# Moving the value products in the attention rounds, and turning two head outputs at a time in the scans

## The chip, the cores and the metric

The kernel runs on one core of one Trainium2 chip. The metric is the device time of one execution in microseconds. Before the change the median of three runs is 2172.1 us (2171.45 to 2173.77). The engines of a core work side by side and wait for each other through semaphores: TensorE (matrix products; PE in the profile, its weight loads PEld), VectorE (DVE), ScalarE (ACT), GpSimd (POOL), and SyncE (SP), whose queue here issues transfers.

## The reference

One encoder layer with two gated branches is applied to a batch of 1024 tokens (called A here) and one of 512 (B), with shared weights and width 1024, all in float32:

```python
h = rms_norm(x, pre_w);  cols = h @ w_in
# branch A: mLSTM with 4 heads of 256, forward and backward, in chunks of 128
num = (sc @ v) + wa * (q @ C);  h_t = num / max(|den|, exp(-m));  C = decay * C + kw.T @ v
y_m = headnorm(h_fwd + h_bwd) * sigmoid(o) * silu(z)
# branch B: 3 dilation groups (1, 4, 16) x 8 heads of 64, window +-64 steps of the dilation
p = exp(q @ k.T + bias - max);  o = p @ v;  y_a = (mix of the groups by their denominators) * silu(z_a)
merged = sig(g0) * (y_m @ w_pm) + sig(g1) * (y_a @ w_pa)
x + rms_norm(merged @ w_out, post_w)
```

## The kernel before

Products in full precision are made of three TensorE products of a high and a low part of each operand (`mm3`, lines 232 to 237). The first 960 us are the input projections of A. After them three kinds of work share TensorE: what A's and B's scans and attention need, step by step, and between these steps *projections* (tile `dense`: B's input projections, then the output projections). The projections come from a generator, `Fill`: `fill(x)` issues a share x of the steps that the stage is to take.

TensorE's and SP's instructions keep the order in which the code writes them (`manual_schedule`). The instructions of ScalarE, VectorE and GpSimd are put in order by a planner that simulates a timeline; `issue_after` ties single instructions behind others, and `self.held` is a list of the last four attention evictions and exponentials, behind which a weight split goes.

The four stages behind the input projections, in time: the scan of A (`mlstm`), the attention of A (`attend`), the scan of B (`quad`, beside which A's attention groups are combined), the attention of B. Then B's groups are combined and the output projections end the kernel.

**Scan rounds.** A round is a head, a chunk and a direction: 4 x 8 x 2 rounds for A, 4 x 4 x 2 for B. In A's round k, TensorE gets in order: a step of `prepare` for the next head, if one is due (six steps, in rounds 8 to 13 of the first three heads: scores `st`, line 1248, or four transpositions of keys, line 1257, each into a PSUM tile `a` that ScalarE empties, lines 1250 and 1258); a `turn`; a third of a share of projections; then `core(k)` with products `num` and `kv` and further projections. From the second half of the chunks on, `core` leaves a normalized head output `hn` (a ring of `late + 1` tiles) and a function `turn` for it: two transpositions into an `a` tile (line 1370), a product with G on VectorE (line 1372) into one of two `ym` tiles, and a write of it that the SP queue issues at the next round's `tick`. `late` is 4 for A and 3 for B: in round k the turn of round k - late runs. Tiles `a` have two PSUM banks, `num` two, `kv` one of two banks; two more are for projections. In B's scan the preparing steps go to another tile (`sc`), and `a` is shared with the combination's transpositions (line 2111). Turns left at the end run one by one with a share of projections each.

**Attention rounds.** `att_round` runs once for each tile of 128 queries and goes through a list of (age, stage): a stage of the tile that came so many rounds ago. Stages of a usual tile: 0 logits `lg` on TensorE (line 1848, or through `mm3`); 1 softmax (VectorE adds the bias and finds the maximum, ScalarE takes exponentials); 2 `turn`, transpositions into `pt` (line 1878) and their copy to `pts` by VectorE or ScalarE in turns; 3 the products with the values, `o`; 4, for A only, transposing back. The list has the place `(None, None)` for a share of projections.

For A, stage 3 is `columns`: only every fourth tile does it, for four tiles at once, with 32 products of 64 output rows (lines 1919 and 1921) and a copy `oT` by ScalarE; stage 4, `back`, turns `oT` (line 1931) and queues the writes. For B, stage 3 is `output`: four to eight products with 64 columns (line 1900; line 1893 for tiles that wrap around), a copy by ScalarE and a queued write for each tile. Tiles of the last dilation group, in both batches, are *compact*: their stages are attached to tiles under other numbers (line 1790), logits (line 1747) as stage 5 of age 0, transpositions (line 1770) as stage 6 of age 4, and their output (line 1779) as stage 3 of age 3. Tiles `lg`, `pt` and `o` have two PSUM banks each.

Of the kernel before, what the change touches and what calls it, by code (L numbers as in the profile page):

```python
# [206 lines left out]
class Net:  # L207
# [1006 lines left out]
    def mlstm(self, T, fill, steps, first, banks, lead, after, beside=()):  # L1214
# [7 lines left out]
        head, made, turns, rws = {0: first}, {}, {}, {}  # L1222
        beside, late = iter(beside), 4 if n > 4 else 3
        self.lag = 2 if n > 4 else 3
        with ExitStack() as stack:
# [150 lines left out]
            def load_G(h):  # L1376
                for c in range(2):
                    self.queue(("G", h), ("G", S, 2 * h + c), G[:, c], T.G[2 * h + c])
# [11 lines left out]
            for k, (h, i, d) in enumerate(rounds):  # L1390
                self.tick()
                if i == (n > 4) and d == (n <= 4):
                    if h < 3:
                        head[h + 1] = self.ml_load(T, h + 1)
                        self.spread(n - 2 if n > 4 else 1)
                    else:
                        after()
                        self.spread(2 * n - 4)
                if d == 0 and i == n // 2 and h < 3:
                    coming = prepare(h + 1)  # L1400
                if coming is not None and next(coming, coming) is coming:
                    coming = None
                if k % 4 < 2:
                    rows(k // 4 + 1, k % 4)
                if k + 1 < len(rounds):
                    with self.tc.issue_after(hold.ins) if k < 3 else ExitStack():
                        front(k + 1)
                self.sum = self.acc[1]
                turns.pop(k - late, lambda: None)()
                if h > 0 and i == 2 and d == 0:  # L1410
                    load_G(h)
                fill(1 / 3)
                core(k)
                self.sum = self.acc[1]
                for _ in range(1 if i < n - 1 else 2):
                    next(beside, None)
# [11 lines left out]
    def quad(self, T, fill, steps, first, after, beside):  # L1428
# [7 lines left out]
        head, made, turns, rws, col = {0: first}, {}, {}, {}, {}  # L1436
        beside, late, lead = iter(beside), 3, 2
        self.lag = 3
        with ExitStack() as stack:
# [157 lines left out]
            for k, (h, i, d) in enumerate(rounds):  # L1597
                self.tick()
                if i == d == 0 and h < 3:
                    qk = self.qk_load(T, h + 1)  # L1600
                    self.spread(1)
                if i == 0 and d == 1:
                    if h < 3:
                        head[h + 1] = self.ml_load(T, h + 1, qk)
                        self.spread(1)
                    else:
                        after()
                        self.spread(2 * n - 4)
                if i == d == 1 and h < 3:
                    coming = prepare(h + 1)  # L1610
                if coming is not None and next(coming, coming) is coming:
                    coming = None
                if k % 4 < 2:
                    rows(k // 4 + 1, k % 4)
                if k + 1 < len(rounds):
                    with self.tc.issue_after(hold.ins) if k < 3 else ExitStack():
                        front(k + 1)
                self.sum = self.acc[1]
                turns.pop(k - late, lambda: None)()
                if h > 0 and i == 2 and d == 0:  # L1620
                    load_G(h)
                fill(1 / 3)
                core(k)
                self.held = []
                self.sum = self.acc[1]
                next(beside, None)
# [98 lines left out]
    def compact(self, T, u, qkv, bias, sb):  # L1725

        nc, n = self.nc, T.n
        q, k, v = qkv
        og = T.og[:, 2, u % 4].rearrange("(i t b) w -> b i t w", t=n, b=2)
        bt = bias()[:, :P].rearrange("p (h w) -> p h w", h=2)  # L1730
        halves = [slice(64 * b, 64 * b + 64) for b in range(2)]
        for hh in range(2):
            e = self.erow[8 * (2 if n > 4 else 3) + 2 * (u % 4) + hh]
            for x in halves:
                self.queue(("table", u), None, bt[x, hh], bass.AP(tensor=e.tensor, offset=e.offset + 193, ap=[[1, 64], [1, 64]]))
        bt = bt[:, :, ::-1]

        def batch(b0):
            ts = {}
            of = lambda t, b: 64 * (2 * (b0 + t) + b)  # L1740

            def products():
                lg = ts["lg"] = self.bank("lg").rearrange("p a b -> p (a b)")
                for t in range(4):
                    for b, x in enumerate(halves):
                        c = slice(of(t, b), of(t, b) + 64)
                        nc.tensor.matmul(lg[x, t * P:(t + 1) * P], q[:, c], k[:, :, c], start=True, stop=True)

            def softmax(i):
                if i == 0:  # L1750
                    ts["st"] = sb.tile([P, 4, 4], F32, name="st", bufs=2)
                    ts["ls"] = sb.tile([P, 2, 256], F32, name="ls", bufs=3).rearrange("p a b -> p (a b)").rearrange(
                        "p (t h w) -> p t h w", t=4, h=2)
                lg = ts["lg"].rearrange("p (t h w) -> p t h w", t=4, h=2)[:, i]
                ls, st = ts["ls"][:, i], ts["st"][:, i]
                nm = sb.tile([P, 2], F32, name="nm", bufs=3)
                for hh in range(2):
                    nc.vector.tensor_tensor_reduce(out=ls[:, hh], in0=lg[:, hh], in1=bt[:, hh], scale=1.0, scalar=NEG, op0=OP.add,
                                                   op1=OP.max, accum_out=st[:, 2 + hh:3 + hh])
                nc.vector.tensor_scalar(nm, st[:, 2:4], -1.0, None, op0=OP.mult)  # L1760
                for hh in range(2):
                    self.held = self.held[-3:] + [nc.scalar.activation(ls[:, hh], ls[:, hh], AF.Exp, bias=nm[:, hh:hh + 1],
                                                                      accum_out=st[:, hh:hh + 1])]

            def turn(i):
                pp = self.bank("pt")
                if i == 0:
                    ts["pt"] = sb.tile([P, 4, P], F32, name="pts", bufs=5 if n > 4 else 2)
                for j in range(2):
                    nc.tensor.transpose(pp[:, j], ts["ls"][:, 2 * i + j].rearrange("p h w -> p (h w)"), self.ident)  # L1770
                pt = ts["pt"][:, 2 * i:2 * i + 2]
                self.held = self.held[-3:] + [nc.scalar.activation(pt, pp[:, :2], AF.Copy) if i else nc.vector.tensor_copy(pt, pp[:, :2])]

            def output():
                po = self.bank("o")
                for t in range(4):
                    for b, x in enumerate(halves):
                        c = of(t, b)
                        nc.tensor.matmul(po[x, t], ts["pt"][:, t, x], v[:, :, c:c + 64], start=True, stop=True)
                if b0 == n - 4 and u < 10:  # L1780
                    self.queued[:0] = self.values_of(T, u + 2, v)
                put = self.ot_batch()
                ot = put.rearrange("p (t w) -> p t w", w=OW)
                nc.vector.tensor_copy(ot[:, :, P:], ts["st"])
                self.held = self.held[-3:] + [nc.scalar.activation(ot[:, :, :P], po, AF.Copy)]
                for b, x in enumerate(halves):
                    self.put(("og", T.S), og[b, :, b0:b0 + 4], ot[x], put, lag=1)

            on = lambda f, *x: (lambda: f(*x))
            return [{6: on(turn, 0)}, {6: on(turn, 1)}, {5: products, 1: on(softmax, 1), 2: on(softmax, 3)},  # L1790
                    {0: on(softmax, 0), 1: on(softmax, 2), 3: output}]

        return [x for b0 in range(0, n, 4) for x in batch(b0)]

    def attention(self, T, u, qkv, bias, sb, ps):
# [257 lines left out]

    def att_round(self, tiles, fill):

        for age, stage in ((0, 0), (1, 1), (2, 2), (4, 4), (None, None), (3, 3), (0, 5), (4, 6)):
            if age is None:
                fill(1)
            elif age < len(tiles) and tiles[-1 - age] is not None and stage in tiles[-1 - age]:
                tiles[-1 - age][stage]()  # L2060
# [1013 lines left out]
```

## Time and profile before

| | |
|---|---|
| median of the runs | 2172.1 us (2171.45 to 2173.77) |
| the profiled execution's own time | 2170.15 us |
| its span, first to last instruction | 2168.4 us |
| TensorE busy | 2153.8 us, 99% |
| VectorE, ScalarE, GpSimd busy | 1495.3, 1105.4, 783.3 us |
| granted TensorE clock | 0.999 |
| scan of A | about 970 to 1304 us |
| attention of A | about 1304 to 1585 us |
| scan of B | about 1585 to 1785 us |
| attention of B | from about 1785 us |

A line of the timeline has the start in us from the span's start, the length in us, the engine, the line of the code, the operation, output tile <- inputs, shapes, and the number of instructions merged; in brackets the idle time of the engine ahead of it and what ended it. Matrix products are pipelined, so that lengths overlap; what an instruction costs TensorE is read from one start to the next. A line of the waits names who waited for whom, the time in all, how often, and the longest. A line of a window has the stretch, its length, and for each engine the busy time and the number of instructions, then the granted clock, the share of the transfer engines and GB/s.

### The profile page before, as it was taken

What the parts mean: (1) busy time and instruction counts of PE and PEld (TensorE: products, weight loads), DVE (VectorE), ACT (ScalarE), POOL (GpSimd) and SP (SyncE); (2) the same over time, 40 slices, a digit from 0 to 9 for tenths busy, and PEclk for the clock granted to TensorE, in tenths of its full rate; (3) what the DMA queues carried; (4) which work ended last, traced back from release to release, by engine and by line L of the source; (5) the groups of instructions that cost most, each with busy time, mean ns of one, the idle gap of its engine ahead of it and who ended that gap; (6) DMA issues with size and microseconds to landing.
All of it is one profiled execution on the core that took longest, in us unless ns stands there. A gap on an engine that the chain in (4) does not pass through costs nothing.

```text
span 2168.4 us, 33777 instructions
## 1 busy us (share of the span) xinstructions
PE 2153.8 (99%) x11530; PEld 1839.3 (85%) x11530; DVE 1495.3 (69%) x2923; ACT 1105.4 (51%) x2286; POOL 783.3 (36%) x1044
## 2 busy tenths in 40 slices
PE   9999999999999999999999999999999999999998
PEld 8988888888888888888888889999788888888886
DVE  8766575658888877536888775565567866676765
ACT  7322344454544444436777666666755544434522
POOL 1000444323333765325776660002025433331332
PEclk9999999999999999999999999999999999999999
DMA  5641687965456554348566548886767879897695
GB/s 217 183 145 57 214 282 242 302 222 187 184 193 218 206 186 176 135 167 291 173 200 221 168 139 261 247 264 186 215 227 250 262 242 332 266 305 221 218 307 141
DMA packets 234517, 469.03 MB, mean 216 GB/s; under 512 B 38281, under 2 KB 120393, under 8 KB 234218
## 3 DMA queue, kind: packets, MB, share of 16 engines
q1 hardware_dynamic: 200600, 345.43, 48.6%
q0 software_dynamic: 30144, 108.86, 15.6%
q10 hardware_dynamic: 3602, 12.59, 1.5%
q8 instruction: 91, 1.49, 0.3%
q14 instruction: 80, 0.66, 0.1%
HBM read 314.56 MB, written 156.43 MB: 217 GB/s over the span
## 4 chain that ended last, share of the span: by engine, by line
PE 97%; ACT 1%; DVE 1%; issue 0%; DMA 0%; SPq 0%; DVEq 0%; POOL 0%; POOLq 0%; ACTq 0%
PE d L235 14%; PE d L237 14%; PE d L236 14%; PE dense L235 13%; PE dense L237 13%; PE dense L236 13%; PE lg L1848 2%; PE pt L1878 2%; PE o L1921 1%; PE num L235 1%; PE num L236 1%; PE num L237 1%; PE num L1541 1%; PE o L1900 1%; PE a L1248 1%; PE kv L235 1%
## 5 line engine op out<-in xcount | busy, mean ns | idle before, releaser
L235 PE MATMUL dense<-H,wh 128*128 128x512 f32 x712 | 288.6, 405 | 0.0
L237 PE MATMUL dense<-H,wl 128*128 128x512 f32 x712 | 279.0, 392 | 0.0
L236 PE MATMUL dense<-H,wh 128*128 128x512 f32 x664 | 260.3, 392 | 0.0
L235 PE MATMUL d<-Hh,phla 128*128 128x512 f32 x608 | 236.5, 389 | 0.0
L237 PE MATMUL d<-Hh,phla 128*128 128x512 f32 x608 | 236.5, 389 | 0.0
L236 PE MATMUL d<-Hl,phla 128*128 128x512 f32 x608 | 236.5, 389 | 0.0
L237 PE MATMUL d<-Hh,phlb 128*128 128x512 f32 x456 | 177.5, 389 | 0.0
L236 PE MATMUL d<-Hl,phlb 128*128 128x512 f32 x456 | 177.4, 389 | 0.0
L235 PE MATMUL d<-Hh,phlb 128*128 128x512 f32 x456 | 177.4, 389 | 0.0
L237 PEld LDWEIGHTS dense<-H,wl 128*128 128x128 f32 x712 | 133.7, 188 | 29.9
L235 PEld LDWEIGHTS dense<-H,wh 128*128 128x128 f32 x712 | 134.1, 188 | 17.7 <-issue 0.9
L305 DVE TENSOR_TENSOR wl<-wraw,wh 128x1024 fp32r<-128x1024 f32 (+1 forms) x95 | 119.7, 1261 | 31.9 <-ACT wh L299 31.9
L785 POOL TENSOR_TENSOR psum_w<-pw_raw 128x512 f32<-128x512 f32 x38 | 52.4, 1380 | 243.9 <-DMA pw_raw<-w_in 120.3
L1867 DVE CUSTOM_DVE_ANT_0 ls<-lg,bias 128x256 f32<-128x256 f32 (+2 forms) x240 | 78.7, 351 | 87.9 <-PE lg L1848 64.0
L236 PEld LDWEIGHTS dense<-H,wh 128*128 128x128 f32 x664 | 125.3, 189 | 14.5
L235 PEld LDWEIGHTS d<-Hh,phla 128*128 128x128 f32 x608 | 114.1, 188 | 23.8
L237 PEld LDWEIGHTS d<-Hh,phla 128*128 128x128 f32 x608 | 114.1, 188 | 23.7
L236 PEld LDWEIGHTS d<-Hl,phla 128*128 128x128 f32 x608 | 114.1, 188 | 23.6
L1871 ACT ACTIVATE ls<-ls,nm 128x256 f32<-128x256 f32 (+1 forms) x192 | 87.4, 456 | 76.2 <-DVE nm L1869 57.9
L235 PE MATMUL d<-v,Hh 128*128 128x484 f32 (+1 forms) x336 | 121.3, 361 | 0.1
L237 PE MATMUL d<-v,Hl 128*128 128x484 f32 (+1 forms) x336 | 120.6, 359 | 0.4 <-DVE Hl L475 0.4
L236 PE MATMUL d<-v,Hh 128*128 128x484 f32 (+1 forms) x336 | 120.2, 358 | 0.3 <-DVE v L500 0.3
(735 smaller groups left out, 5848.7 us busy)
## 6 DMA issues: line engine op xcount, KB each, us to landing
pw_raw<-w_in SPq DMA_DIRECT2D x76, 512.0 KB, 4.2
wraw<-w_in SPq DMA_DIRECT2D x63, 512.0 KB, 4.5
pw_raw<-w_q SPq DMA_DIRECT2D x44, 512.0 KB, 6.3
pre<-phlb SPq DMA_DIRECT2D x32, 512.0 KB, 4.3
aqk_a<-pwk SPq DMA_DIRECT2D x32, 512.0 KB, 7.2
pre<-phlb SPq DMA_DIRECT2D x16, 1024.0 KB, 7.7
wh<-pre POOLq DMA_DIRECT2D x27, 512.0 KB, 6.4
wl<-pre POOLq DMA_DIRECT2D x27, 512.0 KB, 6.7
```

Of the source, the lines that this page charges most:

```text
L235: nc.tensor.matmul(out, lh, rh, start=start, stop=False, **kw)
L236: nc.tensor.matmul(out, lh, rl, start=False, stop=False, **kw)
L237: nc.tensor.matmul(out, ll, rh, start=False, stop=stop, **kw)
L305: low = (self.lows or nc.vector).tensor_sub(lo[:, :n], raw[:, :n], hi[:, :n].bitcast(F32))
L785: self.nc.gpsimd.tensor_add(s[:, 0], ws[1][:, 0], ws[1][:, 1])
L1248: nc.tensor.matmul(p[:, c - c0], kT[:, ct, c * P:(c + 1) * P], qT[:, ct, c * P:(c + 1) * P], start=ct == 0, stop=ct == 1)
L1541: nc.tensor.matmul(pn, hi[:, j], z[:, c1], start=j == 0 and z is v[0], stop=False)
L1848: nc.tensor.matmul(lg[:, hh], q[hh][:, qs], z.rearrange("p (n j) -> p n j", j=P)[:, pair], start=z is k[hh], stop=z is not k[hh])
L1867: nc.vector.tensor_tensor_reduce(out=ls[rows, hh], in0=ts["lg"][hh][rows, of], in1=bt[rows, hh, by], scale=1.0, scalar=NEG, op0=OP.add, op ...
L1871: self.held = self.held[-3:] + [nc.scalar.activation(ls[:, hh], ls[:, hh], AF.Exp, bias=nm[:, hh:hh + 1], accum_out=ot[:, 128 + hh:129 + hh])]
L1878: nc.tensor.transpose(pp[:, hh * nk + x], ts["ls"][:, hh, x * P:(x + 1) * P], self.ident)
L1900: nc.tensor.matmul(po[:, hh * 64:hh * 64 + 64], pt[:, hh * nk + x], vh(kt[x], hh), start=x == 0, stop=x == nk - 1)
```

## The change

Three edits:

1. In both scans a turn no longer runs in each round. In odd rounds k two run, one behind the other: those of rounds k - late - 1 and k - late. Even rounds have none.
2. In `att_round` the entry (3, 3), the products with the values, goes from behind the projections to directly behind the logits of the same round and the softmax of the tile before (which has no TensorE work), ahead of the transpositions (2, 2), (4, 4) and the projections.
3. Where (3, 3) stood, there is now (3, 7), and the compact tiles' output is renamed from stage 3 to stage 7, so that it stays behind the projections.

```diff
@@ mlstm, and the same in quad
                 self.sum = self.acc[1]
-                turns.pop(k - late, lambda: None)()
+                if k % 2:
+                    for a in (k - late - 1, k - late):
+                        turns.pop(a, lambda: None)()
                 if h > 0 and i == 2 and d == 0:
                     load_G(h)
                 fill(1 / 3)
@@ compact
             return [{6: on(turn, 0)}, {6: on(turn, 1)}, {5: products, 1: on(softmax, 1), 2: on(softmax, 3)},
-                    {0: on(softmax, 0), 1: on(softmax, 2), 3: output}]
+                    {0: on(softmax, 0), 1: on(softmax, 2), 7: output}]
@@ att_round
-        for age, stage in ((0, 0), (1, 1), (2, 2), (4, 4), (None, None), (3, 3), (0, 5), (4, 6)):
+        for age, stage in ((0, 0), (1, 1), (3, 3), (2, 2), (4, 4), (None, None), (3, 7), (0, 5), (4, 6)):
```

No instruction is added or removed.

More of the change, by code (lines that the diff above doesn't have):

```diff
@@ L1618, in quad @@
                 self.sum = self.acc[1]
-                turns.pop(k - late, lambda: None)()
+                if k % 2:
+                    for a in (k - late - 1, k - late):
+                        turns.pop(a, lambda: None)()
                 if h > 0 and i == 2 and d == 0:
```

## The prediction

> **What bounds the kernel now.** I read the page first (span, busy shares, chain), then TensorE's own waits, then the sections by window.
>
> ```profile
> span 2168.4 us, 33777 instructions
> PE 2153.8 (99%) x11530; PEld 1839.3 (85%) x11530; DVE 1495.3 (69%) x2923; ACT 1105.4 (51%) x2286; POOL 783.3 (36%) x1044
> PE 97%; ACT 1%; DVE 1%; issue 0%; DMA 0%; SPq 0%; DVEq 0%; POOL 0%; POOLq 0%; ACTq 0%
> ...
> PE pt L1770 <- ACT ls L1762: 1.1, 1, 1.1
> ...
> 960.00:1310.00 350.00, 349.90 (x2072) 307.87 (x2071) 270.05 (x542) 238.69 (x565) 225.36 (x351) 1.00 0.63 208
> ```
>
> TensorE is busy for 99% of the span and is 97% of the chain that ended last. Behind the opening it waits once for another engine, 1.1 us for ScalarE's exponentials. In the first scan (960 to 1310 us; the columns are time, then PE, PEld, DVE, ACT, POOL) it idles 0.1 us of 350. So the kernel's time is the sum of TensorE's instructions, and only two things can move it: what TensorE pays between unlike instructions, and new waits of TensorE. The change removes no instruction. I therefore price its borders between kinds of work, from start to start, and look for waits.
>
> **Attention of the long batch.** Tiles go in fours; every fourth round runs the 32 products with the values (o, 64 columns of the array) behind the projections. Eight units with two groups of four make 16 such rounds.
>
> ```profile
> 1321.86 0.36 PE L236 MATMUL dense<-wl,H 128*128 128x430 f32 x1
> 1322.05 0.35 PE L237 MATMUL dense<-wh,H 128*128 128x430 f32 x1
> 1322.34 1.97 PE L1921 MATMUL o<-pts,K 128*64 128x128 f32 x32
> 1324.23 0.38 PE L1848 MATMUL lg<-V0a,Q 128*128 128x256 f32 x1
> 1324.45 0.28 PE L1848 MATMUL lg<-V0b,Q 128*128 128x256 f32 x1
> 1324.57 0.28 PE L1848 MATMUL lg<-V0a,Q 128*128 128x256 f32 x1
> ...
> 1327.92 0.60 PE L1878 MATMUL pt<-ident,ls 128*128 128x128 f32 x4
> 1328.28 0.44 PE L235 MATMUL dense<-wh,H 128*128 128x430 f32 x1
> ...
> 1501.43 0.61 PE L1921 MATMUL o<-pts,K 128*64 128x128 f32 x8
> 1502.10 1.05 PE L1747 MATMUL lg<-V0a,Q 128*64 128x128 f32 x16
> 1503.08 0.66 PE L1931 MATMUL pt<-ident,oT 128*128 128x128 f32 x4
> 1503.49 0.44 PE L235 MATMUL dense<-wh,H 128*128 128x426 f32 x1
> ```
>
> A projection takes 0.19 us start to start (1321.86 to 1322.05), a logit product 0.12, four transpositions 0.36 (1327.92 to 1328.28), and an o (1.97 - 0.61)/24 = 0.057 with its way in; the same difference for the compact group's logits, which need none, (1.05 - 0.61)/8, gives 0.055. From the last projection at 1322.05 to the second logit product at 1324.45 are 2.40 us; 0.19 + 32 x 0.055 + 0.12 = 2.07 of them are work. So a stay in the 64-column form costs 0.33 us: 0.10 on the way in (0.29 instead of 0.19), some 0.05 in the first pair and the rest, 0.18, on the way out into logits. The way out into transpositions stands once in the trace: 1502.10 to 1503.49 is 1.39, less 16 x 0.055 and 0.36, leaves 0.15.
>
> Before, a round went projections, o, logits, transpositions, projections; after, projections, logits, o, transpositions, projections. The number of ways in and out is the same. 15 rounds change a way out of 0.18 for one of 0.15: **-0.5 us**. The way in from logits is not in the trace. Its bounds are no price at all and the dearest border seen, the 0.22 between the first two logit products behind o (1324.23 to 1324.45, 0.10 over 0.12, and 0.10 before it): I take 0.15, since the instruction ahead is again one that fills all 128 columns. From nothing on both sides to 0.20 on both, 15 rounds give -5.0 to +1.1 us.
>
> The Trainium skill, "TensorEngine Tiling (Array Packing)", section "Key Properties", says that a change of tiling mode drains TensorE. By this rule the change has as many drains as before and its gain here is nil; the trace agrees with the drain (0.33 us a stay) and gives 0.03 us a round beside it.
>
> The 16th round loses something. There o is followed at once by the compact group's logits (1502.10), also in 64 columns. The compact group keeps its own output there (stage renamed to 7), but o of the last wide tiles goes ahead of the projections, so that the two stays separate: one more stay, **+0.35 us**.
>
> Dependencies: the products need the last transposition's copy, in the nearest round
>
> ```profile
> 1464.69 0.36 ACT L1882 ACTIVATE pts<-pt 128x256 f32<-128x256 f32 x1
> 1464.96 0.28 PE L1848 MATMUL lg<-V0a,Q 128*128 128x256 f32 x1
> ```
>
> done at 1465.05, while o could start behind four logit products, 1464.96 + 0.47 = 1465.43, and asks for that tile only with its last eight instructions. No wait. Without this cover a round would lose what the copy is late, at most its 0.36. The moved step also issues ScalarE's copy of o, which the next weight split now queues behind; units are split ahead of use, and the turning back of o gains a round of slack. The output writes hang on a later stage and keep their round.
>
> **Attention of the short batch.** 32 rounds, o in full width:
>
> ```profile
> 1889.17 0.39 PE L237 MATMUL dense<-V0b,wl 128*128 128x512 f32 x1
> 1889.40 0.55 PE L1900 MATMUL o<-X,pts 128*128 128x64 f32 x4
> 1889.76 0.37 PE L235 MATMUL lg<-V1a,Q 128*128 128x256 f32 x1
> 1890.20 0.38 PE L1878 MATMUL pt<-ident,ls 128*128 128x128 f32 x2
> 1890.34 0.48 PE L235 MATMUL dense<-V0b,wh 128*128 128x512 f32 x1
> 1890.66 0.40 PE L236 MATMUL dense<-V0b,wh 128*128 128x512 f32 x1
> ```
>
> 1889.17 to 1890.66 is 1.49; two projections at 0.23, four o at 0.11, three logit products at 0.12 and two transpositions at 0.09 to 0.11 are 1.46 to 1.48. There is at most 0.01 to 0.03 to win: 0 to -0.9 us over 32, I take **-0.1** (the parts stand in one run before and after). The copies come a projection stretch, over 4 us, ahead of need; the writes wait three rounds from the same round as before.
>
> **The scans.** 32 turns of the long batch come in pairs in odd rounds, 16 of the short one nearly so. A single turn:
>
> ```profile
> 1053.72 0.28 PE L237 MATMUL num<-ch,ql 128*128 128x258 f32 x1
> 1053.84 0.38 PE L1370 MATMUL a<-ident,hn 128*128 128x128 f32 x2
> 1053.97 0.49 PE L235 MATMUL dense<-H,wh 128*128 128x512 f32 x1
> 1054.30 0.39 PE L236 MATMUL dense<-H,wh 128*128 128x512 f32 x1
> ```
>
> From 1053.72 to 1054.30 is 0.58; 0.12, two at 0.11 (1048.62 to 1049.06 below is four) and 0.23 are 0.57: a visit costs 0.01 us. Visits saved: three in each of three heads, two in the last, one in each of three heads of the short batch, 14 in all: **-0.15 us**.
>
> Now the waits. A turn takes one of two PSUM banks "a". So does each step that prepares the next head, and the last of these runs in the head's round 13, directly ahead of the turns. Before, round 13 had one turn: two banks. After, it has a preparing step and two turns: the third must wait until ScalarE has emptied the first's bank (L1258). These are the three heads' steps and copies:
>
> ```profile
> 1048.62 0.60 PE L1257 MATMUL a<-ident,K 128*128 128x128 f32 x4
> 1049.06 0.38 PE L1370 MATMUL a<-ident,hn 128*128 128x128 f32 x2
> 1127.83 0.60 PE L1257 MATMUL a<-ident,K 128*128 128x128 f32 x4
> 1205.86 0.60 PE L1257 MATMUL a<-ident,K 128*128 128x128 f32 x4
> ...
> 1046.84 1.05 ACT L299 ACTIVATE wh<-wraw 128x1024 fp32r<-128x1024 f32 x1
> 1047.79 0.58 ACT L924 ACTIVATE sw<-dense 128x512 fp32r<-128x512 f32 x1
> 1050.40 0.58 ACT L1258 ACTIVATE K<-a 128x512 f32<-128x512 f32 x1
> 1128.76 0.58 ACT L1258 ACTIVATE K<-a 128x512 f32<-128x512 f32 x1
> 1206.83 0.58 ACT L1258 ACTIVATE K<-a 128x512 f32<-128x512 f32 x1
> ```
>
> The second turn would start six transpositions (0.65 us) behind the step: 1049.27, 1128.48, 1206.51. The copies end at 1050.98, 1129.34, 1207.41: waits of 1.71, 0.86 and 0.90, **+3.5 us**. Behind the waiting transposition stand the round's projections and its num and kv products, that is all of TensorE, and with 0.1 us idle in 350 nothing makes it up. Least: ScalarE free at once, the copy ending 0.58 behind the step's 0.60, leaves 0.5 each, 1.6 us. Most: each copy behind a split and an eviction (1.05 + 0.58) too, 3.5 + 4.9 = 8.4.
>
> Elsewhere the banks suffice: pairs are two rounds apart. The hn ring has five places (four in the short batch) and the longest queue of unturned heads is five (four). Half of the ym writes leave a round later, two at a time, from SP's queue, which has waited for them before; weight and key loads are queued behind.
>
> ```profile
> SPq L251 <- DVE ym L1372: 25.9, 11, 5.1
> ...
> ACT wh L299 <- DMA wraw<-w_v: 4.1, 1, 4.1
> ```
>
> ScalarE waited for a weight once in this section, so loads run ahead; I cost this at nothing. If that cover went, an odd round would lose up to the one wait seen, 4.1.
>
> **The sum**: -0.5 + 0.35 - 0.1 - 0.15 + 3.5 = +3.1 us. The profiled execution took 2170.15 us (span 2168.4, 1.75 around it), 1.95 under the median of 2172.1; the terms are differences, so I add them to the median: **2175.2 us**.
>
> **Rivals.**
>
> *No new wait* (the bank is given out otherwise, or ScalarE's order puts the copy first and early). For it: the planner orders ScalarE anew and may see TensorE stand. Against: the copy stood behind four or five other instructions in all three heads, and even at once leaves 0.5 each. Then -0.4: 2171.7 us, the change doing next to nothing.
>
> *Slower: the copy behind the split.* In head 0 a split and an eviction are in the queue just ahead (1046.84, 1047.79). If the new order puts them between the step and its copy, each stall grows by 1.63: 8.4 - 0.4 = +8.0, 2180.1 us. It decides from a copy that ends over 2 us behind the step. Against: the split stood ahead of the copy in no head but as work already done.
>
> *Faster: no drains between logits, o and transpositions.* If the parts between the projections cost nothing at their borders, -5.0 + 0.35 - 0.25, without stalls 2167.2 us. Against it stands the 0.15 of 1503.08 to 1503.49.
>
> **How the numbers follow.** My forecast 0.46, no new wait 0.21, slower 0.23, faster 0.10. A measurement of this kernel can tell about 0.2%, 4.3 us, from no change: 2167.8 to 2176.4. The forecast's own range is 2173.3 (least stalls) to 2177.5 (0.8 us more in each of the three waits); a fifth of it (0.09) lies above 2176.4. Slower: 0.23 + 0.09 = 0.32, less what of the slower case stays under the bound (0.03): 0.29. Faster 0.10, the same 0.61. The range leaves out the faster case's end and the slower one's: 2168 to 2181.
>
> **What would show it.** Right: TensorE's waits list a new one for L1258 at L1370, three times, 0.5 to 1.7 us each; L1370's visits fall from one in each round to one in two; behind o stands pt with a gap near 0.15; the short batch's rounds stay at 1.49. Wrong: no such wait; or logits to o without the 0.10; or a wait in the attention rounds at o or pt; or stalls over 2 us.

## The result, and the profile after

The changed kernel takes 2181.8 us (median of 6 runs, 2180.5 to 2184.0) against 2172.6 us (6 runs, 2171.5 to 2173.8) of the kernel before on the same chip: a ratio of 1.0042, 95% interval 1.0032 to 1.0052. It is slower by about 9.2 us, more than the 4.3 us that a measurement can tell from no change. Forecast were 2175.2 us, with a range from 2168 to 2181, counted from the earlier median of 2172.1.

Where the 9 us are is seen from four stages. The lengths in this document run from one start of a TensorE instruction to another: the scan of A from its first product into `a` to the last turn, the attention of A from there to its last `o`, the scan of B from the first `sc` to the last turn, the attention of B from there to its last `o`. The two fences below are the windows of these stages, before and after (start and end, length, then busy time and instructions of PE, PEld, DVE, ACT, POOL, then granted clock, share of the transfer engines, GB/s).

```profile
971.73:1303.94 332.21, 332.11 (x1984) 292.86 (x1983) 259.81 (x515) 228.66 (x546) 218.89 (x345) 1.00 0.62 202
1303.94:1582.71 278.77, 277.62 (x2149) 251.67 (x2147) 168.39 (x715) 183.91 (x566) 27.85 (x51) 1.00 0.78 230
1593.24:1767.05 173.81, 173.81 (x905) 147.09 (x904) 130.15 (x331) 95.22 (x212) 85.31 (x144) 1.00 0.73 241
1767.05:2027.89 260.84, 260.84 (x1429) 220.83 (x1427) 165.22 (x471) 116.35 (x353) 79.12 (x147) 1.00 0.82 275
```

```profile
972.62:1308.61 335.99, 332.50 (x1984) 293.00 (x1983) 260.85 (x515) 228.84 (x546) 218.39 (x345) 1.00 0.61 200
1308.61:1586.74 278.13, 276.99 (x2148) 253.11 (x2147) 169.71 (x715) 183.11 (x566) 27.48 (x51) 1.00 0.80 231
1597.27:1776.02 178.75, 175.24 (x904) 148.25 (x903) 128.78 (x331) 95.67 (x212) 80.56 (x144) 0.99 0.71 234
1776.02:2038.30 262.28, 260.33 (x1428) 219.19 (x1427) 163.74 (x471) 116.42 (x353) 79.14 (x147) 1.00 0.82 274
```

Length less PE's busy time is what TensorE stood still. Before, that is 0.10, 1.15, 0 and 0 us; after, 3.49, 1.14, 3.51 and 1.95. The stages change by +3.8, -0.6, +4.9 and +1.4 us, +9.5 in all. The opening took 0.9 us longer in this execution (the first window starts at 972.62 instead of 971.73); in the profiles of all kernels of this document, which share the opening, it varies between 971.6 and 973.8, so this is not the change's.

TensorE's waits in the changed kernel name the causes, in us in all, times, longest. Shown are those behind the opening:

```profile
PE num L1543 <- ACT sch L1529: 3.5, 1, 3.5
PE a L1370 <- ACT K L1258: 3.3, 3, 1.8
...
PE dense L236 <- DVE H L2298: 1.2, 1, 1.2
PE pt L1774 <- ACT ls L1766: 1.1, 1, 1.1
...
PE dense L235 <- DVE mg L2462: 0.8, 1, 0.8
```

The wait for L1258 was forecast. The 1.1 us at `pt` were there before. The other three, 5.5 us in all, were not forecast.

**The scan of A.** Head 0, round 13 in the timelines of TensorE and of ScalarE:

```profile
1049.08 0.60 PE L1257 MATMUL a<-ident,K 128*128 128x128 f32 x4
1049.51 0.38 PE L1370 MATMUL a<-ident,hn 128*128 128x128 f32 x2
1051.68 0.44 PE L1370 MATMUL a<-ident,hn 128*128 128x128 f32 x2 [1.78 <-ACT K L1258]
1051.87 0.49 PE L235 MATMUL dense<-H,wh 128*128 128x512 f32 x1
...
1051.05 0.57 ACT L1258 ACTIVATE K<-a 128x512 f32<-128x512 f32 x1
```

The third tile `a` of the round waits until ScalarE has emptied the first.

**The scan of B.** Head 0, round 11: SP's queue, then VectorE, ScalarE and TensorE.

```profile
1652.68 1.16 SPq L276 DMA_DIRECT2D V0a<-vs_b  x2
...
1655.10 1.20 SPq L251 DMA_DIRECT2D ym_b<-ym  x2
...
1664.19 0.42 DVE L1575 TENSOR_TENSOR ym<-a,X 128x256 f32<-128x256 f32 x1 [4.08 <-DMA ym_b<-ym]
1664.61 1.20 DVE L305 TENSOR_TENSOR wl<-wraw,wh 128x1024 fp32r<-128x1024 f32 x1
1666.33 0.28 DVE L1521 TENSOR_TENSOR rm<-rm,st 128x128 f32<-128x128 f32 x1
...
1666.65 0.52 ACT L1529 ACTIVATE sch<-rm 128x384 fp32r<-128x384 f32 x1 [1.45 <-DVE rm L1521]
...
1667.22 1.66 PE L1543 MATMUL num<-V1a,sch 128*128 128x258 f32 x6 [3.52 <-ACT sch L1529]
1668.67 0.63 PE L235 MATMUL dense<-H,wh 128*128 128x512 f32 x1
1669.10 0.63 PE L236 MATMUL dense<-H,wh 128*128 128x512 f32 x1
```

The two writes of a pair are issued from 1655.10 on, behind two loads. VectorE's next product of a turn needs a place of the two `ym` tiles and waits 4.08 us for a write to land. Behind it in VectorE's queue stand a weight split and `rm`; ScalarE's `sch` waits for `rm`, TensorE's `num` for `sch`. TensorE had work until then and stands still for 3.52 us.

What follows is a second price. From 1668.67 to 1669.10 a projection takes 0.43 us instead of 0.23. The window of that stretch and one behind it:

```profile
1667.20:1670.30 3.10, 3.08 (x11) 2.76 (x12) 3.10 (x6) 0.88 (x2) 2.35 (x4) 0.53 0.94 289
1672.00:1676.00 4.00, 4.00 (x22) 3.41 (x21) 3.24 (x15) 3.57 (x10) 1.92 (x5) 1.00 1.01 348
```

The granted clock is 0.53 in the 3 us behind the stall, then 1.00 again (the last section shows where it changes). So the stage loses 4.94 us: 3.51 still, and 1.43 more busy time for the same instructions (175.24 instead of 173.81).

**The attention of B.** TensorE waits twice, and VectorE once in the chain of the first wait:

```profile
1921.63 0.29 DVE L1871 CUSTOM_DVE_ANT_0 ls<-lg,bias 128x128 f32<-128x128 f32 x1 [1.64 <-DMA og_b<-ot]
1922.06 0.69 DVE L2298 TENSOR_TENSOR H<-ymr,H 128x512 fp32r<-128x512 f32 x1
...
1922.80 0.50 PE L236 MATMUL dense<-H,wh 128*128 128x512 f32 x1 [1.18 <-DVE H L2298]
...
1928.04 0.50 PE L235 MATMUL dense<-H,wh 128*128 128x512 f32 x1 [0.78 <-DVE mg L2462]
```

A softmax waits for the write of an output tile `ot`; behind it on VectorE stands the low part of an operand of the next projections.

**A round of A's attention** with `o` at its new place:

```profile
1324.04 0.36 PE L237 MATMUL dense<-wh,H 128*128 128x430 f32 x1
1324.24 0.28 PE L1852 MATMUL lg<-V0a,Q 128*128 128x256 f32 x1
...
1324.59 0.28 PE L1852 MATMUL lg<-V0b,Q 128*128 128x256 f32 x1
1324.80 1.97 PE L1925 MATMUL o<-pts,K 128*64 128x128 f32 x32
1326.70 0.66 PE L1882 MATMUL pt<-ident,ls 128*128 128x128 f32 x4
1327.11 0.44 PE L235 MATMUL dense<-wh,H 128*128 128x430 f32 x1
```

From 1324.04 to 1327.11 are 3.07 us. A projection of 0.19, four logit products of 0.12, 32 products at 0.055 and 0.36 for the transpositions are 2.79. The stay in the 64-column form costs 0.28 instead of 0.33. Its way in from logits is 0.21 - 0.12 = 0.09, about that from projections (0.10). What is cheaper is the first work behind it: transpositions take 0.41 instead of 0.36, 0.05 more, where before the first logit product took 0.22 instead of 0.12, 0.10 more.

### The profile page after: what moved, and what is told of

Read it like the earlier page. It is cut to its first block, busy times and chain, and to the rows that moved or that the text cites. A ratio compares the mean times of both kernels' runs of the same rounds, so it can differ in the third digit from the quotient of the medians.

```text
span 2178.7 us, 33768 instructions
## 1 busy us (share of the span) xinstructions
PE 2155.0 (99%) x11530; PEld 1840.6 (84%) x11530; DVE 1495.7 (69%) x2923; ACT 1105.3 (51%) x2286; POOL 778.7 (36%) x1044
## 4 chain that ended last, share of the span: by engine, by line
PE 60%; DMA 3%; issue 2%; POOL 2%; DVE 2%; ACT 1%; DVEq 0%; POOLq 0%; SPq 0%; ACTq 0%
PE dense L235 11%; PE dense L236 11%; PE dense L237 11%; PE d L237 4%; PE d L236 4%; PE d L235 4%; PE lg L1852 2%; PE pt L1882 2%; PE o L1925 1%; PE num L235 1%; PE num L236 1%; PE num L237 1%; PE num L1543 1%; PE kv L235 1%; PE a L1248 1%
## 5 line engine op out<-in xcount | busy, mean ns | idle before, releaser
L299 ACT ACTIVATE wh<-wraw 128x1024 fp32r<-128x1024 f32 (+1 forms) x98 | 100.9, 1031 | 39.8 <-PE dense L236 25.3
```

The costliest lines, as they stand in the source:

```text
L299: high = nc.scalar.activation(hi[:, :n], raw[:, :n], AF.Copy)
```

## The experiments

The theory behind the first four: the scans lose by waits that pairs bring (in A for the third `a` tile, in B for a `ym` tile), and the attention edit is worth little by itself. The rival for B's scan: two turns in a row are too much for VectorE whatever the number of `ym` tiles. Lengths of the stages in us, from the profiles; the last column is the median of the timed runs, beside 2172.3 to 2172.6 of the kernel before:

| kernel | scan A | attention A | scan B | attention B | sum of four | time |
|---|---|---|---|---|---|---|
| before | 332.2 | 278.8 | 173.8 | 260.8 | 1045.6 | 2172.3 |
| after | 336.0 | 278.1 | 178.8 | 262.3 | 1055.2 | 2181.8 |
| B's scan single | 337.0 | 278.1 | 173.8 | 262.9 | 1051.8 | 2176.5 |
| four `ym` tiles in B's scan | 336.8 | 278.1 | 173.7 | 263.0 | 1051.6 | 2176.0 |
| attention edit alone | 333.2 | 278.1 | 173.8 | 261.4 | 1046.5 | 2171.4 |
| pairs alone | 336.8 | 278.8 | 179.5 | 261.0 | 1056.1 | 2181.6 |
| pairs of A in even rounds, B single | 336.1 | 278.4 | 177.0 | 258.3 | 1049.8 | 2175.2 |
| A's attention alone | 332.9 | 278.1 | 174.5 | 260.8 | 1046.3 | 2171.8 |
| two stays a group | 336.8 | 283.0 | 179.4 | 265.2 | 1064.5 | 2187.5 |
| pairs with the waits mended | 335.5 | 278.7 | 173.7 | 258.6 | 1046.4 | 2172.7 |

**B's scan back to single turns.** In the changed kernel, `quad` alone:

```diff
-                if k % 2:
-                    for a in (k - late - 1, k - late):
-                        turns.pop(a, lambda: None)()
+                turns.pop(k - late, lambda: None)()
```

> Changed kernel, but the short batch's scan turns one output in each round again. Theory (a wait of VectorE for the write of an ym tile, caused by the pair of rounds 9 and the turn of round 11): the 3.5 us wait of TensorE for num behind VectorE's 4.1 us wait goes, and the projections at 0.43 us behind it; the short scan (first sc product to last turn) falls from 178.8 to about 173.8 us, the time by 4.9 us to about 2177. Rival (the planner's new order of the other engines as a whole, with pairs or without): the short scan stays within 1 us of 178.8 or stalls elsewhere. The long scan keeps its three waits, 336.0 us, by both.

Measured: 2176.5 us, ratio to the kernel before 1.0021 (1.0012 to 1.0031). The window of B's scan:

```profile
1597.28:1771.07 173.79, 173.79 (x905) 147.16 (x903) 129.95 (x331) 95.12 (x212) 83.75 (x144) 1.00 0.72 240
```

TensorE never stands still, and the stage is as long as before. The pairs of B's scan are the cause there, worth 5 us of the 9.

**Pairs kept in B's scan, with four `ym` tiles.** The two further tiles are the unused columns of two buffers of the combination. The line that makes the ring, the rest of the edit left out:

```diff
@@ combine, beside B's scan
...
+            self.ym_of = Rot(self, [b[F32] for b in old.bufs] + [x[:, 1600:1856] for x in whole])
...
```

> Changed kernel, pairs kept, but in the short batch's scan the ring of ym tiles has four places instead of two (the two more lie in unused columns of two tiles that the combination of the long batch holds). Theory (the ring's two places and their slow writes): VectorE's 4.1 us wait for the write goes with the pairs left in, the short scan falls to about 174 us, the time to about 2177. Rival (the pairs themselves: two products of VectorE in a row, or two transposition pairs, delay num): the short scan stays near 178.8.

Measured: 2176.0 us, ratio 1.0021 (1.0011 to 1.0031).

```profile
1597.28:1770.97 173.69, 173.69 (x904) 147.16 (x903) 128.87 (x331) 95.58 (x212) 83.60 (x144) 1.00 0.73 241
```

The pairs are still there and cost nothing. So two turns in a row do not stall the scan by themselves; they do with two places for the turns' results. (What in the timing made a pair wait where single turns did not is a reading: a pair takes both places at once, and both of their writes left together behind loads.)

**The attention edit alone**, both scans with single turns:

> Only the attention edit of the change; both scans as before. Theory: scans as before (332.2 and 173.8 us); the long attention keeps its gain of 0.6 us (278.1); the short attention shows whether its two waits of 1.35 and 0.94 us come from the edit: with them 262.3, without them about 260.0, that is 0.85 under before. Time 2170 to 2173. Rival (the attention edit makes those waits by itself, planner's order): 262.3 us in the short attention and a time above 2172.6.

Measured: 2171.4 us, ratio 0.9995 (0.9985 to 1.0004): the same as before. A's attention gains 0.64 us, as in the changed kernel; B's loses 0.5, which this window of it shows:

```profile
1767.82:2029.19 261.37, 260.22 (x1429) 219.41 (x1427) 163.73 (x471) 116.36 (x353) 79.14 (x147) 1.00 0.82 275
```

TensorE's busy time in B's attention falls by 0.62 us (260.84 to 260.22), but 1.15 us of waits stand where there was none.

**The pairs alone**, the attention as before:

> Only the paired turns; attention as before. Theory: long scan 336.0 us with three waits for the preparing step's copy (3.3 us in all), short scan 178.8 with the ym wait, attentions 278.8 and 260.8 as before; time 2172.6 + 3.8 + 4.9 = 2181. Rival (the stalls need both edits, since the planner's order hangs on all): the sum of this run's and the attention run's differences does not come to the whole change's 9.2.

Measured: 2181.6 us, ratio 1.0042 (1.0027 to 1.0057). The whole loss is there without the attention edit, and the two parts add up within what these measurements tell: (2171.4 - 2172.5) + (2181.6 - 2172.5) = +8.0 of the changed kernel's +9.3.

**A's pairs in even rounds**, B's scan single:

```diff
@@ mlstm
-                if k % 2:
+                if k % 2 == 0:
```

> The kernel after with two edits: in the long batch's scan the pairs of turns run in even rounds, in the short batch's scan turns run one at a time as before. Theory (the three waits of the long scan come from a preparing step and two turns in the same round 13, three PSUM tiles 'a' out of two banks): in even rounds the pair meets a preparing step at rounds 8, 10 and 12, but when the first turns of a head fall due, in round 12, only one is there, so no round asks for three tiles. No wait of TensorE for L1258 at L1370; first scan 332.2 us as before, less about 0.1, instead of 336.0; the time near that of the attention edit alone, 2171.4 us. Rival (turning two in a row delays the scan in itself, by the order of ScalarE and VectorE, and the round does not matter): three waits remain somewhere in the scan, 336 us, time 2175.2 to 2176.5.

Measured: 2175.2 us, ratio 1.0011 (1.0002 to 1.0020), 3.8 us over what the theory gave. TensorE's waits in A's scan, and the windows of A's scan, B's scan and B's attention:

```profile
PE num L235 <- ACT X L1345: 1.1, 2, 0.6
...
973.42:1309.49 336.07, 334.87 (x1996) 295.32 (x1995) 261.05 (x516) 230.16 (x547) 216.84 (x344) 1.00 0.60 199
1598.44:1775.42 176.98, 175.24 (x904) 146.75 (x903) 129.24 (x329) 94.94 (x213) 81.38 (x141) 1.00 0.74 243
1775.42:2033.70 258.28, 257.50 (x1416) 217.14 (x1415) 163.94 (x471) 116.08 (x353) 77.94 (x147) 1.00 0.81 274
```

The wait for L1258 is gone, which is what the theory said of its cause. (Of the 1.1 us for L1345, 0.6 stands at a place where the two kernels with A's scan unchanged stand still too, 0.6 us with the attention edit alone and 0.5 with A's attention alone; the other 0.5 does not occur there.) The length of the stage alone would have misled: A's scan holds 12 instructions more (1996, not 1984), and B's attention 12 fewer (1416, not 1428). In even rounds five turns are left at the scan's end instead of four, and each goes with a share of projections, so that 12 projection products, some 2.8 us at 0.23, moved from one stage to the other. Without them A's scan is 333.3 us.

The miss lies in B's scan, with single turns at 177.0 us instead of 173.8. TensorE stood still there for 1.7 us, and its busy time was 1.4 us longer at a granted clock of 1.00; the cause of the longer busy time is open. VectorE waited in front of the same product:

```profile
1663.36 0.42 DVE L1575 TENSOR_TENSOR ym<-a,X 128x256 f32<-128x256 f32 x1 [2.04 <-DMA ym_b<-ym]
```

In the kernel before, VectorE's waits in B's scan have for this only:

```profile
DVE ym L1573 <- DMA ym_b<-ym: 0.8, 1, 0.8
```

So two `ym` tiles are short for single turns too: 0.8 us there, 2.0 here. The other kernels with single turns in B's scan have such waits of 0.5 to 1.4 us in all, without a stall of TensorE over 0.3 us. That the 2.0 us are what TensorE stood still for is read from the timeline; it was not tried.

**A's attention alone moved**: the attention edit, and besides it this line, by which B's output stays behind the projections. Both scans are single:

```diff
-            return dict(enumerate((products, softmax, turn, columns, back) if by_four else (products, softmax, turn, output)))
+            return dict(enumerate((products, softmax, turn, columns, back))) if by_four else {0: products, 1: softmax, 2: turn, 7: output}
```

> The kernel before with the products with the values moved ahead of transpositions and projections in the long batch's attention only; the short batch's output stays behind its projections, and both scans turn one at a time. Theory (the short batch's attention loses by waits that the move there brings, 2.3 us in the kernel after, against 0.85 gained): long attention 278.1 us instead of 278.8, short attention 260.8 us as before with no wait of TensorE in it; the time 0.6 us under the kernel before, 2171.9 us. Rival (the waits in the short batch's attention come from what the long batch's attention leaves behind): waits of TensorE for L2294 or L2458 of 1 to 2 us remain and the short attention takes 261.4 us or more.

Measured: 2171.8 us, ratio 0.9997 (0.9988 to 1.0005).

```profile
971.70:1304.61 332.91, 332.23 (x1985) 292.98 (x1983) 260.10 (x515) 228.92 (x546) 219.53 (x345) 1.00 0.61 202
...
1767.74:2028.56 260.82, 260.82 (x1429) 220.92 (x1427) 164.53 (x471) 116.39 (x353) 79.11 (x147) 1.00 0.82 275
```

B's attention has no wait of TensorE: those of the changed kernel come from moving B's own output. That the softmax's wait for an `ot` write is their cause is read from the timeline; it was not tried. A's attention takes 278.1 us again. A's scan, whose program up to its end is that of the kernel before, came out 0.7 us longer here, and 1.0 us with the attention edit alone, where it is the same program too. So a scan of this kernel can differ by that much between two executions, and a smaller difference of one profile says nothing.

**Two stays a group.** In the changed kernel a group of four tiles does its 32 products in two parts:

```diff
@@ columns
-                if slot < 3:
+                if slot % 2 == 0:
                     return
-                po = self.bank("o").rearrange("p a b -> p (a b)")
+                if slot == 1:
+                    batch["po"] = self.bank("o").rearrange("p a b -> p (a b)")
+                po = batch["po"]
...
-                for t in range(4):
+                for t in (slot - 1, slot):
...
```

> The kernel after, but in the long batch's attention a usual group of four tiles does its 32 products of 64 output rows in two parts of 16, at its second and its fourth tile, into the same PSUM tile; the number of products, copies and transpositions is as in the kernel after, only the number of stays in the 64-column form doubles, 16 more. Theory (what a round pays at the borders is paid for each stay, about 0.28 us between logits and transpositions): long attention 278.1 + 16 x 0.28 = 282.6 us, and the time 4.5 us over the kernel after, 2186.3 us. Rival (the border costs nothing, the time belongs to the products themselves): long attention 278.1 us, 2181.8 us. In between, the measured price of a stay is the difference divided by 16.

Measured: 2187.5 us, ratio 1.0066 (1.0050 to 1.0081). The window of A's attention:

```profile
1308.46:1591.48 283.02, 281.87 (x2148) 253.67 (x2147) 171.50 (x715) 183.46 (x566) 27.48 (x51) 1.00 0.77 227
```

It is 4.89 us longer for the same instructions, 0.31 us for each of 16 stays. The border has a price of its own. B's attention took 2.9 us more than in the changed kernel, because its wait for `H` was 2.75 us here, with slow projections behind it (last section).

**Pairs with the waits mended**: A's in even rounds, B's with four `ym` tiles, and the move in A's attention alone.

> Pairs of turns in both scans without the waits that they brought: in the long scan in even rounds, in the short scan with four ym tiles instead of two; the products with the values moved in the long batch's attention only. Theory (all that pairs gain is 0.01 us a visit, 14 visits, and the move gains 0.64 us): long scan 332.1 us, long attention 278.1, short scan 173.7, short attention 260.8 us; 0.8 us under the kernel before, 2171.7 us, which a measurement cannot tell from no change. Rival (pairs gain more than the visits once nothing waits): the two scans together are over 1 us shorter than the 332.2 + 173.8 of before, and the time is under 2170.5 us.

Measured: 2172.7 us, ratio 1.0001 (0.9993 to 1.0010). With the waits away the pairs gain nothing that shows: the four stages sum to 1046.4 against 1045.6. (A's attention kept only 0.1 of its 0.64 us here; why is open.) No kernel tried is faster than the one before by more than a measurement can tell.

## Why the prediction was wrong

The sign of the sum was right, and so was the largest of its terms. Its size was a third of what came, because a part of the change was costed at nothing.

- **The step that failed** is the prediction's "Half of the ym writes leave a round later, two at a time, from SP's queue, which has waited for them before; weight and key loads are queued behind", with "I cost this at nothing". It looked at what is queued behind the writes on SP. The waiter was on the other side: VectorE, which needs the place that the write frees. With a ring of two, B's scan lost 4.94 us; with four, nothing. That "ScalarE waited for a weight once" was no cover for that: it is another buffer, another engine and another scan. The rings of `hn` and the banks were counted, the ring of `ym` was not. The bound of 4.1 us stood in the text without a place in the range; that VectorE's wait was 4.08 us is chance, since the 4.1 was ScalarE's wait for a weight. The prediction's own sign of being wrong, "stalls over 2 us", came.
- **Clock behind a stall.** The prediction costed a wait at its length. The stall of 3.52 us cost 1.43 us more at a granted clock of 0.53. None of the stalls it forecast was long enough to show this: behind the 1.78 us two transpositions take 0.19 us (1051.68 to 1051.87), no more than elsewhere.
- **The three waits in A's scan**: +3.5 forecast, 3.3 measured (1.78, 0.74 and 0.80, against 1.71, 0.86 and 0.90). Mechanism, place and size held, and even rounds took the wait away.
- **A's attention**: -0.5 + 0.35 = -0.15 forecast, -0.64 measured in five kernels alike (the changed one, and the first three and the sixth of the experiments), but -0.4 and -0.1 in the two with A's pairs in even rounds. A round gains 0.05 by the lines above, or some 0.07 by the length of the stage if the sixteenth round paid its 0.35, instead of 0.03. The way in was taken as unchanged, and is; the gain lies on the way out. The price of a stay held (0.33 before, 0.28 after, 0.31 by doubling).
- **B's attention**: -0.1 forecast, within 0 to -0.9. TensorE's busy time fell by 0.5 to 0.6 us, inside the bounds. But "The copies come a projection stretch, over 4 us, ahead of need" covered the products alone. What came late was the operand of a projection, behind a softmax on VectorE, and the stage lost 1.4 us.
- **Visits**: -0.15 forecast; the mended kernel shows no gain of that or any other size.
- **The rivals.** "The copy behind the split" named 2180.1 us, near the truth, by a mechanism that didn't occur: the longest of the three stalls was 1.78 us and no split stood between a step and its copy. "No new wait" and "no drains" fell with the waits and with the 0.31 us a stay.

The terms as measured: 3.8 in A's scan, -0.6, 4.9 and 1.4 make 9.5, against 9.2 between the medians. The 3.1 of the forecast lacked the 4.9 of B's scan and 1.5 of B's attention.

## What to carry to other kernels

When two steps are put together that ran one at a time, count every ring that they pass, up to the last one whose place comes free only when a transfer has landed, and price a wait at the far end through the in-order engine that would stand: here a product of 0.42 us held up TensorE over two other engines. Where TensorE is busy for 99% of the span, a wait that an engine off the path took before without harm (0.8 us) is the row to look at, for it says how little slack there is. Compare stages of two kernels with their instruction counts beside them, or work that has merely moved will look like a cost.

## What was not expected of the hardware

A stall of TensorE costs more than its length once it is long. In the kernel with two stays a group, as in the changed kernel, projections are slow behind one:

```profile
1929.78 0.79 PE L236 MATMUL dense<-H,wh 128*128 128x512 f32 x1 [2.75 <-DVE H L2302]
1930.38 0.63 PE L237 MATMUL dense<-H,wl 128*128 128x512 f32 x1
1930.80 0.63 PE L235 MATMUL dense<-K,wh 128*128 128x512 f32 x1
```

From 1930.38 to 1930.80 a projection takes 0.42 us. The slow stretch does not begin where the stall ends. These are its windows in the changed kernel, in the pairs alone (whose stall of 3.95 us in B's scan ends at 1670.38), and twice in the kernel with two stays (a stall of 3.12 us in B's scan ends at 1672.37, the one above at 1929.78):

```profile
1666.72:1670.13 3.41, 2.91 (x10) 2.63 (x11) 3.41 (x7) 1.33 (x3) 2.31 (x3) 0.50 0.96 264
...
1670.38:1670.93 0.55, 0.55 (x4) 0.55 (x5) 0.55 (x3) 0.26 (x1) 0.53 (x1) 1.00 1.03 216
1670.93:1674.34 3.41, 3.41 (x12) 2.83 (x11) 2.89 (x5) 1.10 (x3) 2.03 (x4) 0.50 1.01 337
...
1673.46:1676.87 3.41, 3.41 (x11) 2.84 (x10) 2.74 (x8) 0.92 (x2) 1.98 (x4) 0.50 1.06 375
...
1929.46:1932.87 3.41, 3.09 (x7) 2.48 (x8) 1.27 (x4) 0.88 (x4) 0.00 (x0) 0.50 1.08 243
```

The half clock lasts 3.41 us each time, whatever the stall's length, and begins up to 0.5 us before the stall's end or up to 1.1 us behind it. What it costs is half of TensorE's busy time in it: 2.91 / 2 = 1.46 us in the changed kernel, where the busy time grew by 1.43. In the three others it is 1.7, 1.7 and 1.5, where the stage's busy time grew by 1.8, 2.3 and 1.4; the 0.6 that the second of them has over is open. The changes of the clock keep to steps: in each of the ten profiles every one lies a whole number of 3.413 us behind the first (in the changed kernel 11.26, then 1666.72 and 1670.13, which are 485 and 486 steps). In the step that ended with the halving TensorE had stood still for 3.0, 2.9, 2.3 and 2.4 us, in the order of the fence; the longest stall behind the opening without a halving is 1.79 us, within one step. Where between 1.79 and 2.3 us the bound lies is open.

The Trainium skill, "TensorE: Matmul & The Clock Gate", section "Part 1: The HAM clock gate", puts the halving down to an idle window of about 3.4 us and the return to a busy one of about that length. The length of the half clock, 3.41 us, agrees; the halving came with 2.3 to 3.0 us of standing still in a step.

The landing of a small write varies: `ym` tiles of 128 KB landed between 1.8 and 9.0 us after their issue, with a median of 2.2. The pair that VectorE waited for had been issued behind loads; that the loads made it late is not shown. This is the row of the tile in the changed kernel:

```profile
DMA to landing us min/median/max: 1.8/2.2/9.0
```
